# A 3x3 convolution on one core: dealing output channels to partitions so that sixteen DMA engines store neighbouring channels

## The chip, the core and the metric

The kernel runs on one core of a Trainium2 chip. The core has a matrix engine (TensorE, PE in the profile), a vector engine (VectorE, DVE), a scalar engine (ScalarE, ACT), a general engine (GpSimd, POOL) and SyncE (SP), which in this kernel issues every transfer. Transfers between the chip's memory and the on-chip memory of 128 partitions are carried out by sixteen DMA engines that work beside the others. The metric is the device time of one execution in microseconds (us); less is better. The median of three executions of the kernel before is 126.97 us (126.95 to 127.01).

## The reference

The inputs are 16 images of 64 channels with 64 x 64 points, and the weights of a 3 x 3 convolution from 64 to 128 channels, all in 32-bit floats:

```
x: (16, 64, 64, 64)      weight: (128, 64, 3, 3) * 0.1
x_pad = pad(x, one zero on each side of h and w)
output[b, co] += weight[co, ci, kh, kw] * x_pad[b, ci, kh:kh+h, kw:kw+w]     (sum over ci, kh, kw)
output: (16, 128, 64, 64), float32
```

The input holds 16.8 MB and the output 33.6 MB. One channel of one image is 64 x 64 x 4 = 16,384 bytes, and lies in one piece in memory; the channels of an image follow each other.

## The kernel before

**Tiling.** Two images make a pair `p` (0 to 7); their 2 x 64 input channels fill the 128 partitions. Each pair is worked on in two halves `h` of 32 output rows, so there are sixteen steps of the main loop (line 221). The rows are transformed in the manner of Winograd along the height: two output rows come from sums and differences of input rows (`ss`, `dd`, `ee`, made on GpSimd two steps ahead; `xh`, a cast to 16 bits on ScalarE) and combined weights `Wt`. TensorE multiplies for the two images of a pair with 64 rows each, and the products for image `b2` land in an accumulator of 128 output channels. VectorE (lines 247 to 251) and ScalarE (lines 192 and 253) put the four parts together in the output tile `ov[b2]`, whose partition is the output channel.

**Weights.** The first transfer (line 59) loads the weights as 128 rows of 2,304 bytes, row `co` into partition `co` of `w_raw`. They are cast, transposed by matmuls with an identity (line 102) and combined to `Wt`. Which output channel sits in which partition of the accumulators, and then of the output tiles, follows from which weight row was loaded into which partition of `w_raw`.

**Loads.** Pair 0 comes in two transfers (34 and 30 rows), pairs 1 and 2 in one each, pairs 3 and 4 together in one transfer into a double tile `two` (line 81). Pairs 5, 6 and 7 are loaded later, when a tile comes free (`NEXT_LOADS`): after the steps (1, 1), (3, 0) and (4, 0).

**Homes.** `X_HOME` and `O_HOME` say in which of five single and two double tiles a pair's input and outputs lie. An output tile is used again for a later pair, so the later pair's results wait until the earlier store has landed.

**Stores.** After the second half of a pair `store` (line 204) issues its stores. For the pairs in `BOTH` (0, 3 and 6) one transfer stores both images: for each partition, the channel of the first image and then that of the second, 2 MB further on. The other pairs are stored by two transfers of 128 channels. One image, the second of pair 5, is cut (`FEW`): its first 57 rows go as usual, and its last 7 rows are stored by a transfer of 124 partitions and one of 4, so that the packets are 7 x 64 x 4 = 1,792 bytes.

**What sets the order.** `keep` fixes each engine's instructions in the order of the text. All transfers are issued by SyncE in that order: a transfer that waits for results holds up those behind it. The DMA engines work each through its own list of packets in the order of issue. The completion of a transfer is told by one of eight flags that the framework takes in turn, so that a transfer also waits until the one eight places before it has landed. The order of transfers is: weights, pair 0 in two parts, 1, 2, 3 and 4; stores of pairs 0 and 1; load of 5; store of 2; load of 6; store of 3; load of 7; stores of 4, 5, 6, 7.

Of the kernel before, what the change touches and what calls it, by code (L numbers as in the profile page):

```python
# [15 lines left out]
def kernel(  # L16
# [12 lines left out]
    nc = tc.nc  # L29
    B, CI, H, W = x.shape  # L30
    CO = weight.shape[0]
# [3 lines left out]

    keep = tc.keep_in_program_order
    x_rows = x.rearrange("b c h w -> (b c) h w")
    w_flat = weight.rearrange("co ci kh kw -> co (ci kh kw)")

    const = ctx.enter_context(tc.tile_pool(name="const", bufs=1))  # L40
    psum = ctx.enter_context(tc.tile_pool(name="psum", bufs=8, space=bass.MemoryType.PSUM))
# [6 lines left out]

    X_HOME = [0, 1, 2, ("d", 0), ("d", 1), 2, ("d", 0), ("d", 1)]
    O_HOME = ["b", (3, 4), (0, 1), "b", (3, 4), (0, 1), "b", (2, 3)]  # L50
    BOTH = (0, 3, 6)
    FEW = 5, 1, 7
    NEXT_LOADS = {(1, 1): 5, (3, 0): 6, (4, 0): 7}

    def home(k, name):
        return slots.tile([128, H, W], F32, tag=f"s{k}", name=name)

    w_raw = const.tile([CO, CI * 9], F32)
    keep(nc.sync.dma_start(w_raw, w_flat))
    xs = {}  # L60

    def load(p, cuts=((0, H),)):
        if X_HOME[p] in range(5):
            xs[p] = home(X_HOME[p], "xs")
        for lo, hi in cuts:
            keep(
                nc.sync.dma_start(
                    xs[p][:, lo:hi, :], x_rows[128 * p : 128 * p + 128, lo:hi, :]
                )
            )  # L70

    two = slots.tile([128, 2, H, W], F32, tag="d", name="two")
# [4 lines left out]
    load(0, ((0, 34), (34, H)))  # L77
    load(1)
    load(2)
    rows = x_rows[128 * 3 : 128 * 5, :, :].rearrange("(g p) h w -> p g h w", g=2)  # L80
    keep(nc.sync.dma_start(two, rows))

    ident = const.tile([128, 128], F16)
    make_identity(nc, ident)
# [45 lines left out]
    def cast(p, h):  # L130
        t = cpool.tile([128, 17, W], F16, tag="xh", name="xh")
        keep(nc.scalar.copy(t, xs[p][:, C_ROW[h] : C_ROW[h] + 17, :]))  # L132
        return t

    def transforms(eng, p, h):
        return sums(eng, p, h), diffs(eng, p, h), outers(eng, p, h)
# [17 lines left out]
    def mms(tiles, terms, start, stop):  # L154
        n = 3 * len(terms)
        i = 0
        for wi, src, row in terms:
            for kw in (1, 0, 2):
                c_lo, c_hi = max(0, 1 - kw), min(W, W + 1 - kw)
                lo, hi = 0, RB  # L160
                at, step, rows = row
                while at + step * lo < 0:
                    lo += 1
                while at + step * (hi - 1) > rows - 1:
                    hi -= 1
                first, last = at + step * lo, at + step * (hi - 1)
                for b2 in range(2):
                    p0 = 64 * b2
                    keep(
                        nc.tensor.matmul(  # L170
                            tiles[b2][:, lo:hi, c_lo:c_hi],
                            Wt[p0 : p0 + 64, wi, kw, :],
                            src[
                                p0 : p0 + 64,
                                first : last + 1 : step,
                                c_lo + kw - 1 : c_hi + kw - 1,
                            ],
                            start=start and i == 0,
                            stop=stop and i == n - 1,
                            skip_group_check=not start,  # L180
                        )
                    )
                i += 1

    def acc():
        return [psum.tile([128, RB, W], F32, tag="acc", name="acc") for _ in range(2)]

    def copies(tiles):
        us = []
        for b2 in range(2):  # L190
            ut = upool.tile([128, RB, W], F32, tag="ut", name="ut")
            keep(nc.scalar.copy(ut, tiles[b2]))  # L192
            us.append(ut)
        return us
# [3 lines left out]
    def outputs(p):  # L198
        if O_HOME[p] == "b":
            both = slots.tile([128, 2, H, W], F32, tag="b", name="both")  # L200
            return both, [both[:, b2, :, :] for b2 in range(2)]
        return None, [home(k, "ot") for k in O_HOME[p]]

    def store(p, both, ots):
        if p in BOTH:
            pair = out[2 * p : 2 * p + 2, :, :, :].rearrange("b c h w -> c b h w")
            keep(nc.sync.dma_start(pair, both))
            return
        for b2 in range(2):
            parts = [(0, CO, 0, H)]  # L210
            if (p, b2) == FEW[:2]:
                at = H - FEW[2]
                parts = [(0, CO, 0, at), (0, 124, at, H), (124, 4, at, H)]
            for c, n, lo, hi in parts:
                keep(
                    nc.sync.dma_start(
                        out[2 * p + b2, c : c + n, lo:hi, :], ots[b2][c : c + n, lo:hi, :]
                    )
                )

    for n, (p, h) in enumerate(halves):
        if n + 2 < len(halves):
            tr[halves[n + 2]] = transforms(nc.gpsimd, *halves[n + 2])
        if h == 0:
            both, ots = outputs(p)
            ov = [t.rearrange("p (j i) c -> p j i c", i=2) for t in ots]
        ss, dd, ee = tr.pop((p, h))
        xc = xh.pop((p, h))
        jf, jg = RB * F_BLK[h], RB * G_BLK[h]
        sf, sg = jf - 16 * h, jg - 16 * h  # L230
        g_at = 2 * jg - C_ROW[h]

        pf1, pg1, pf2, pg2 = acc(), acc(), acc(), acc()
        mms(pf1, [(HP, ss, (sf, 1, 16))], True, True)
        ux = copies(pf1)
        mms(pg1, [(G1, ss, (sg, 1, 16))], True, True)
        ug = copies(pg1)
        mms(pf2, [(HM, dd, (0, 1, RB))], True, True)
        uy = copies(pf2)
        if n + 1 < len(halves):  # L240
            xh[halves[n + 1]] = cast(*halves[n + 1])
        mms(pg2, [(G01, xc, (g_at, 2, 17)), (G2, xc, (g_at + 2, 2, 17))], True, True)
        mms(pf1, [(G0, ee, (0, 2, 16))], False, True)
        mms(pg1, [(G21, xc, (g_at + 1, 2, 17)), (G0, xc, (g_at - 1, 2, 17))], False, True)
        mms(pf2, [(G2, ee, (1, 2, 16))], False, True)
        for b2 in range(2):
            keep(nc.vector.tensor_add(ov[b2][:, jg : jg + RB, 1, :], pg2[b2], ug[b2]))  # L247
        for b2 in range(2):
            keep(nc.vector.tensor_add(ov[b2][:, jf : jf + RB, 0, :], pf1[b2], uy[b2]))  # L249
        for b2 in range(2):  # L250
            keep(nc.vector.tensor_sub(ov[b2][:, jf : jf + RB, 1, :], ux[b2], pf2[b2]))  # L251
        for b2 in range(2):
            keep(nc.scalar.copy(ov[b2][:, jg : jg + RB, 0, :], pg1[b2]))  # L253
        if h == 1:
            store(p, both, ots)
        if (p, h) in NEXT_LOADS:
            load(NEXT_LOADS[p, h])

# [29 lines left out]
```

## Time and profile before

| what | value |
|---|---|
| median of three executions | 126.97 us |
| the profiled execution | 127.13 us |
| its span (first to last instruction) | 125.4 us |
| PE, DVE, ACT, POOL busy | 95.6, 66.8, 85.4, 90.5 us |
| moved | 50.78 MB, mean 405 GB/s |
| read from, written to memory | 17.07 MB, 33.55 MB |
| transfers issued by SyncE | 24: 9 loads (the weights among them), 15 stores |

The page gives busy time by engine, the span in 40 slices (a digit is a tenth of a slice; the row DMA is the mean of the sixteen DMA engines, GB/s what they moved), the DMA queues, and the chain of work that ended last. The queue q1 carries the kernel's transfers; q8 and q14 carry the engines' program code. Beside the page the trace holds a record of every packet that a DMA engine moved, with start, duration and size; in this kernel a packet of a whole channel has 16,384 bytes. The completion of a transfer shows as sixteen packets of 4 bytes, one on each engine that took part.

### The profile page before, as it was taken

How to read it: one execution, taken by the hardware profiler on the slowest of the kernel's cores; microseconds unless marked ns; L12 is line 12 of the kernel's file. 1: busy time of each engine (PE TensorE's matmuls, PEld its weight loads, DVE VectorE, ACT ScalarE, POOL GpSimd, SP SyncE). 2: the span in 40 equal slices, each digit the busy share in tenths (PEclk: the TensorE clock that was granted, in tenths of full speed). 3: DMA queues.
4: the chain of work that ended last, by engine and by line, in shares of the span. 5: the costliest groups of instructions: out<-in, count | busy, mean ns of one | idle time of the engine just before them, and what ended most of it. 6: DMA issues, size and time to landing. Idle time of an engine off the chain costs nothing.

```text
span 125.4 us, 2343 instructions
## 1 busy us (share of the span) xinstructions
PE 95.6 (76%) x873; PEld 48.9 (39%) x873; DVE 66.8 (53%) x104; ACT 85.4 (68%) x150; POOL 90.5 (72%) x52
## 2 busy tenths in 40 slices
PE   0349999999999999999999999999999960000000
PEld 0223555555455555555555555555555520000000
DVE  0199658393939476574939394765749390000000
ACT  4458598989797988989897979789898930000000
POOL 2209999999999999999999999999999300000000
PEclk9999999999999999999999999999999996555555
DMA  4999999999999999999999999999999999999971
GB/s 132 371 453 423 434 424 439 423 335 418 434 431 429 426 434 418 423 429 434 416 439 424 423 423 423 418 431 434 423 424 423 433 416 443 423 429 444 418 335 47
DMA packets 3827, 50.78 MB, mean 405 GB/s; under 512 B 360, under 2 KB 488, under 8 KB 744
## 3 DMA queue, kind: packets, MB, share of 16 engines
q1 hardware_dynamic: 3816, 50.63, 96.2%
q8 instruction: 7, 0.11, 0.3%
q14 instruction: 4, 0.03, 0.1%
HBM read 17.07 MB, written 33.55 MB: 404 GB/s over the span
## 4 chain that ended last, share of the span: by engine, by line
PE 76%; DMA 2%; DVE 2%; POOL 1%; DVEq 0%; ACT 0%; issue 0%
PE acc L170 75%; DMA w_raw<-in_weight_dram 2%; DVE ss L114 1%; DVE ot L251 1%; POOL w L87 1%; DVEq L283 0%; DVE th L141 0%; DVE Wt L142 0%; PE wp L102 0%; ACT g0h L139 0%; DVEq L142 0%
## 5 line engine op out<-in xcount | busy, mean ns | idle before, releaser
L170 PEld LDWEIGHTS <-Wt 64*128 64x128 f16 x864 | 48.0, 96 | 48.5 <-issue 3.0
L192 ACT COPY ut<-acc 128x512 f32<-128x512 f32 x96 | 48.7, 612 | 4.4 <-PE acc L170 4.4
L170 PE MATMUL acc<-xh,Wt 64*128 64x504 f16 (+3 forms) x384 | 46.2, 372 | 0.0
L170 PE MATMUL acc<-ss,Wt 64*128 64x504 f16 (+1 forms) x192 | 24.8, 392 | 2.3 <-DVE ss L114 2.3
L170 PE MATMUL acc<-ee,Wt 64*128 64x504 f16 (+1 forms) x192 | 26.4, 377 | 0.0
L247 DVE TENSOR_TENSOR ot<-acc,ut 128x512 f32<-128x512 f32 x20 | 12.9, 686 | 20.0 <-ACT ut L192 15.8
L114 POOL TENSOR_TENSOR ss<-xs 128x1024 f16<-128x1024 f32 x7 | 16.6, 2366 | 4.7 <-DMA xs<-in_x_dram 4.7
L127 POOL TENSOR_TENSOR ee<-two 128x1024 f16<-128x1024 f32 x8 | 19.0, 2378 | 0.0
L114 POOL TENSOR_TENSOR ss<-two 128x1024 f16<-128x1024 f32 x8 | 19.0, 2369 | 0.0
L127 POOL TENSOR_TENSOR ee<-xs 128x1024 f16<-128x1024 f32 x7 | 16.6, 2376 | 0.0
L253 ACT COPY ot<-acc 128x512 f32<-128x512 f32 x20 | 10.7, 589 | 5.5 <-PE acc L170 5.5
L170 PE MATMUL acc<-dd,Wt 64*128 64x504 f16 (+1 forms) x96 | 13.9, 392 | 0.0
L247 DVE TENSOR_TENSOR both<-acc,ut 128x512 f32<-128x512 f32 x12 | 7.7, 686 | 11.0 <-ACT ut L192 7.9
L251 DVE TENSOR_TENSOR ot<-ut,acc 128x512 f32<-128x512 f32 x20 | 12.8, 682 | 0.2
L249 DVE TENSOR_TENSOR ot<-acc,ut 128x512 f32<-128x512 f32 x20 | 12.8, 680 | 0.0
L121 POOL TENSOR_TENSOR dd<-two 128x512 f16<-128x512 f32 x8 | 10.3, 1287 | 0.0
L121 POOL TENSOR_TENSOR dd<-xs 128x512 f16<-128x512 f32 x7 | 10.0, 1423 | 0.0
L132 ACT CAST xh<-two 128x1088 f16<-128x1088 f32 x8 | 9.3, 1157 | 0.0
L132 ACT CAST xh<-xs 128x1088 f16<-128x1088 f32 x8 | 9.2, 1145 | 0.0
L253 ACT COPY both<-acc 128x512 f32<-128x512 f32 x12 | 6.4, 589 | 3.5 <-PE acc L170 3.5
L251 DVE TENSOR_TENSOR both<-ut,acc 128x512 f32<-128x512 f32 x12 | 7.7, 683 | 0.1
L249 DVE TENSOR_TENSOR both<-acc,ut 128x512 f32<-128x512 f32 x12 | 7.7, 680 | 0.0
(23 smaller groups left out, 14.9 us busy)
## 6 DMA issues: line engine op xcount, KB each, us to landing
out_dram<-ot SPq DMA_DIRECT2D x9, 2048.0 KB, 18.5
out_dram<-both SPq DMA_DIRECT2D x3, 4096.0 KB, 22.5
xs<-in_x_dram SPq DMA_DIRECT2D x3, 2048.0 KB, 16.2
two<-in_x_dram SPq DMA_DIRECT2D x1, 4096.0 KB, 28.4
two<-in_x_dram SPq DMA_DIRECT2D x2, 2048.0 KB, 23.1
out_dram<-ot SPq DMA_DIRECT2D x1, 1824.0 KB, 24.3
xs<-in_x_dram SPq DMA_DIRECT2D x1, 1088.0 KB, 5.4
xs<-in_x_dram SPq DMA_DIRECT2D x1, 960.0 KB, 7.4
```

The costliest lines, as they stand in the source:

```text
L87: keep(nc.gpsimd.tensor_copy(w16[:, 0, :], w_raw))
L114: keep(eng.tensor_add(t, v[:, j : j + 16, 0, :], v[:, j : j + 16, 1, :]))
L121: keep(eng.tensor_sub(t, v[:, j : j + RB, 1, :], v[:, j : j + RB, 0, :]))
L127: keep(eng.tensor_sub(t, xs[p][:, r - 1 : r + 15, :], xs[p][:, r + 1 : r + 17, :]))
L132: keep(nc.scalar.copy(t, xs[p][:, C_ROW[h] : C_ROW[h] + 17, :]))
L170: nc.tensor.matmul(tiles[b2][:, lo:hi, c_lo:c_hi], Wt[p0 : p0 + 64, wi, kw, :], src[p0 : p0 + 64, first : last + 1 : step, c_lo + kw - 1 : ...
L192: keep(nc.scalar.copy(ut, tiles[b2]))
L247: keep(nc.vector.tensor_add(ov[b2][:, jg : jg + RB, 1, :], pg2[b2], ug[b2]))
L249: keep(nc.vector.tensor_add(ov[b2][:, jf : jf + RB, 0, :], pf1[b2], uy[b2]))
L251: keep(nc.vector.tensor_sub(ov[b2][:, jf : jf + RB, 1, :], ux[b2], pf2[b2]))
L253: keep(nc.scalar.copy(ov[b2][:, jg : jg + RB, 0, :], pg1[b2]))
```

## The change

- Weight row `16 j + e` is loaded into partition `8 e + j` (e from 0 to 15, j from 0 to 7), so partition `8 e + j` of every output tile holds output channel `16 j + e`.
- A store of an image is written as 16 x 8 channels in memory, `e` outside and `j` inside, from 128 partitions. If a DMA engine takes one `e`, that is eight neighbouring partitions, then at its step `j` the sixteen engines store the sixteen neighbouring channels `16 j` to `16 j + 15`.
- No transfer stores a pair: pairs 0, 3 and 6 are stored by two transfers each as well. Pairs 3 and 4 are loaded by two transfers.
- The images of the last pair are stored in two halves of 32 rows each (`HALVED`), by transfers of 8,192-byte packets.
- The last 7 rows of pair 5's second image are stored by four transfers of 4 x 8 channels (32 partitions each) instead of 124 and 4 partitions.

```diff
-    w_flat = weight.rearrange("co ci kh kw -> co (ci kh kw)")
+    w_dealt = weight.rearrange("(j e) ci kh kw -> e j (ci kh kw)", e=16)
...
-    BOTH = (0, 3, 6)
+    HALVED = (7,)
...
-    keep(nc.sync.dma_start(w_raw, w_flat))
+    keep(nc.sync.dma_start(w_raw, w_dealt))
...
-    rows = x_rows[128 * 3 : 128 * 5, :, :].rearrange("(g p) h w -> p g h w", g=2)
-    keep(nc.sync.dma_start(two, rows))
+    load(3)
+    load(4)
...
-            return both, [both[:, b2, :, :] for b2 in range(2)]
-        return None, [home(k, "ot") for k in O_HOME[p]]
-
-    def store(p, both, ots):
-        if p in BOTH:
-            pair = out[2 * p : 2 * p + 2, :, :, :].rearrange("b c h w -> c b h w")
-            keep(nc.sync.dma_start(pair, both))
-            return
-        for b2 in range(2):
-            parts = [(0, CO, 0, H)]
+            return [both[:, b2, :, :] for b2 in range(2)]
+        return [home(k, "ot") for k in O_HOME[p]]
+
+    def store(p, ots):
+        for b2 in range(2):
+            to = out[2 * p + b2].rearrange("(j e) h w -> e j h w", e=16)
+            cuts = [0, 32, H] if p in HALVED else [0, H]
             if (p, b2) == FEW[:2]:
-                at = H - FEW[2]
-                parts = [(0, CO, 0, at), (0, 124, at, H), (124, 4, at, H)]
-            for c, n, lo, hi in parts:
+                cuts = [0, H - FEW[2]]
+            for lo, hi in zip(cuts, cuts[1:]):
+                keep(nc.sync.dma_start(to[:, :, lo:hi, :], ots[b2][:, lo:hi, :]))
+
+            for g in range(0, 16, 4) if cuts[-1] < H else ():
                 keep(
                     nc.sync.dma_start(
-                        out[2 * p + b2, c : c + n, lo:hi, :], ots[b2][c : c + n, lo:hi, :]
+                        to[g : g + 4, :, cuts[-1] : H, :],
+                        ots[b2][8 * g : 8 * g + 32, cuts[-1] : H, :],
                     )
                 )
...
-            store(p, both, ots)
+            store(p, ots)
```

More of the change, by code (lines that the diff above doesn't have):

```diff
@@ L224 @@
         if h == 0:
-            both, ots = outputs(p)
+            ots = outputs(p)
             ov = [t.rearrange("p (j i) c -> p j i c", i=2) for t in ots]
```

## The prediction

> **What bounds the kernel now.** I read the page's slices first, then the chain of waits, then SyncE's waits, then the windows, and last the trace's records of single DMA packets.
>
> ```profile
> span 125.4 us, 2343 instructions
> ...
> DMA  4999999999999999999999999999999999999971
> GB/s 132 371 453 423 434 424 439 423 335 418 434 431 429 426 434 418 423 429 434 416 439 424 423 423 423 418 431 434 423 424 423 433 416 443 423 429 444 418 335 47
> ...
> q1 hardware_dynamic: 3816, 50.63, 96.2%
> q8 instruction: 7, 0.11, 0.3%
> ```
>
> The DMA engines are full from the second slice to the last but one; no compute engine is busy after slice 33. The chain's last pieces and SyncE's waits say the same:
>
> ```profile
> 8.00 94.44 PE acc L170 x864
> 102.44 0.68 DVE ot L251
> 103.12 0.60 DVEq L283
> ```
>
> ```profile
> SPq L283 <- DMA out_dram<-ot: 9.9, 3, 4.8
> SPq L283 <- DMA out_dram<-both: 9.6, 1, 9.6
> SPq L67 <- ACT xh L132: 7.9, 3, 3.0
> ```
>
> The last result is computed at 103.1 us, the last store issued right after, and the remaining 21 us are SyncE at the end of the program waiting for stores. TensorE's 76% of the span is beside the point: what ends the kernel is 50.63 MB through sixteen DMA engines. The windows give their rate by stage (last column GB/s, the one before the engines' busy share):
>
> ```profile
> 2.00:8.00 6.00, 1.15 (x9) 1.02 (x10) 2.30 (x4) 2.69 (x6) 0.66 (x1) 1.00 1.00 381
> 8.00:26.00 18.00, 18.00 (x149) 8.80 (x150) 12.89 (x19) 14.58 (x27) 16.86 (x9) 1.00 1.02 434
> 26.00:29.00 3.00, 3.00 (x32) 1.59 (x30) 2.90 (x5) 2.34 (x5) 3.00 (x2) 1.00 0.99 322
> 29.00:47.00 18.00, 18.00 (x172) 9.24 (x170) 11.21 (x18) 16.02 (x30) 18.00 (x10) 1.00 1.01 430
> 68.00:76.00 8.00, 8.00 (x78) 4.08 (x76) 4.93 (x8) 7.12 (x14) 8.00 (x5) 1.00 0.99 420
> 82.00:103.00 21.00, 20.41 (x192) 10.29 (x188) 14.23 (x23) 17.46 (x32) 16.28 (x9) 1.00 1.01 427
> 104.00:118.00 14.00, 0.00 (x0) 0.00 (x0) 0.00 (x0) 0.00 (x0) 0.00 (x0) 0.52 1.01 432
> ```
>
> Loads alone run at 434, stores alone at 430 to 432. The packet records say why: the median 16 KB packet takes 611 ns in every stage, load or store (all 365 that start from 8 to 22 us, 329 of 367 from 104 to 118), and the next starts 4 ns before it ends, so one per 607 ns per engine, 27.0 GB/s, 432 for sixteen. A store already moves at an engine's own pace, wherever its channels lie. What is not at that pace: the 3 us around 28 us, where the first loads end and the first store begins, lose (432 - 322) x 3 / 432 = 0.76 us; the windows from 29 to 103 us lose 0.86 us together by the same working; and the engines end apart, their last completions lying between 120.2 and 124.2 us with a mean of 122.1. The late one fits seven fetches of TensorE's code (the q8 line, 16 KB each, 0.88 to 1.04 us, each beside one data packet stretched to about 1.0 to 1.1): 7 x 0.607 = 4.2 us against a spread of 4.0.
>
> **The change part by part.** The profiled execution took 127.13 us (span 125.4 and 1.8 around it), 0.16 above the median of 126.97. The sum is made on it and the 0.16 taken off.
>
> *Same work.* All matmuls, copies and transforms stay, in the same order on their engines. Weight rows are permuted as they are loaded, so a result lands in another partition at the same instruction. Bytes are the same. These cost nothing, and need no cover.
>
> *Weight load.* Still 128 rows of 2,304 B, now 36,864 B apart for one engine. It heads the DMA queue and the chain (0.74 to 3.69 us), so a delay moves everything. Records: median 93 ns, worst 552. Bounds: one such worst packet more or less, plus or minus 0.46 us; I take 0, since each engine's first packets are slow now (164 to 552 ns) and the sixteen rows of one step are neighbours as well.
>
> *Pairs 3 and 4 loaded by two transfers instead of one, pairs 0, 3 and 6 stored by two instead of one, the last two images by two halves each.* Six more transfers on all sixteen engines. The end of a transfer costs an engine 6 ns: the completions of consecutive loads lie 4.862 us apart for 8 packets of 607 ns (4.856). 6 x 6 = 0.04 us. The halved images have 8 KB packets: the records have 328 ns for 8,704 B and 291 for 7,680, so 309.5 for 8,192; two are 619 against 611. Starts lie 4 ns closer, so between 3.4 and 8 ns for each of 16 packets; I take 3.4, the start-to-start value: 0.05 us.
>
> *The seven rows that four engines store alone.* Before 31 + 1 packets of 1,792 B on each, after 4 x 8 = 32; two more transfer ends, 0.01 us. The 128 packets took 74 ns each, and this share stays.
>
> *Issues.* Eight more transfers on SyncE, at 0.39 us each (the three-dimensional store of a pair took 383 to 405 ns, against 356 for a plain one): 3.1 us. SyncE waits 78 us for VectorE at its stores, and the queue it feeds is 10 to 20 us deep (18.5 us median from issue to landing): hidden. At its thinnest, pair 1's store is issued at 34.14 us, 3.8 us before pair 0's is through at 37.9. The last four issues end near 105.5 us; the first engine is through with the previous pair at 110.4: cover 4.9 us.
>
> *Waits.* Eight completion flags are taken in turn, so each transfer waits for the one eight before it. More transfers make that one a later one. The tight ones, by landings in the trace: the fourth piece of the seven rows waits for the load of pair 7 (last engine 85.8 us; issued before at about 82.8); pair 6's second image waits for pair 4's second (95.5, against 92.27); the last pair's second half for pair 5's second image (104.7, against 103.2). Behind each on SyncE stand only later stores, and nothing computes from them. Each comes over 4 us before an engine could use it: 0. Output tiles are reused no later: pair 6 needs pair 3's store, landed by 80.9 us, as before.
>
> *Where a store reads and writes.* This is the substance, and the trace of before does not show it. On the memory side the sixteen engines now fill 256 KB without gaps at a step. The nearest rows: loads of the same rows at 434 GB/s, stores at 432. Since both are at the engine's pace, a better pattern can take away only the excess listed above: at most 0.76 + 0.86 = 1.62 us. A worse one is bounded by the slowest 8 us of the trace, 420 against 432 GB/s: 33.55 MB of stores, 77.7 us, times 2.8% = 2.2 us, of which about 0.6 is paid already: 1.6 us. I take 0, between equal ends and nearest to the 611 ns median. On the on-chip side each engine should now read eight neighbouring partitions. Nearest row: the seven rows. Four engines sweep over 31 partitions each, between 100.9 and 103.9 us, while the others read their own partitions; every small packet took 74 ns, and of 97 large packets then in flight 85 took their usual 545 or 611. Reading near another engine cost nothing there, for short stretches.
> [...]
>
> The sum: 127.13 + 0.04 + 0.05 + 0.01 = 127.23, less 0.16: 127.07; I say 127.1.
>
> **The rivals.**
> *The stall at the switch shrinks (faster).* In its favour: the stall is shared by nearly all engines at once (29 packets between 25.9 and 29.2 us took over 660 ns), and stores by pair alternate between two images 2 MB apart, which stops. Against: it falls on the last two packets of the loads, which the change leaves, and later switches (near 52, 67 and 82 us) cost little. Half of the 1.62 us gone: 127.07 - 0.8 = 126.3.
> *Neighbouring blocks get into each other's way in memory (slower).* Place: every store packet. Price: half the bound, 0.8 us, so 127.9. It decides from 2 ns on each of an engine's 128 store packets (0.25 us). For it: some store packets from 30 to 47 us already take 640 to 660 ns (mean 615.4). Against: the loads from 8 to 22 us read neighbouring rows with no slow packet at all.
> *Two engines share a way out of on-chip memory (much slower).* Place: every store of all sixteen engines. If the shared way carries what one engine moves, a packet takes 2 x 607 ns and the 77.7 us of stores double: 205 us; engines that drift four packets apart would escape it, and the late one is six or seven behind. Against: the 74 ns. [...]
> *The split is another one.* If an engine gets other partitions than eight neighbours, a step stores some groups of channels apart. The time is then the forecast's.
>
> **How the numbers follow.** No change apart from the 0.1 us, with the other split in it: 0.34, range 126.8 to 127.3. Stall shrinks: 0.26. Memory conflict: 0.30. Shared way: 0.10. A measurement of this kernel tells from no change about 0.2%, 0.25 us. So faster 0.26, same 0.34, slower 0.40. The range 126.2 to 128.4 leaves out the shared way (0.10), the upper end of the memory conflict (0.03) and the best part of the gain (0.06).
>
> **What would show it.** Right: 16 KB store packets with a median of 611 ns, 8 KB near 309; 104 to 118 us still at about 432 GB/s; 26 to 29 near 322; SyncE's last waits still on stores of some 20 us. Wrong: store stages under 425 (conflict) or near 216 (shared way), packets of 1.2 us; 26 to 29 us above 380 (gain); TensorE with gaps before 102 us, which would mean that a flag wait or a late load reached the computation.

## The result: 10.5% slower, and the profile after

The changed kernel takes 140.99 us (median of six executions, 139.63 to 143.62), the kernel before on the same chip 126.99. The ratio is 1.105, with a 95% interval of 1.099 to 1.111. Medians here and below are of all executions, while ratios leave out those more than 1.5% above the fastest of their kernel, here two of the six. The forecast was 127.1 with a range from 126.2 to 128.4: wrong. The profiled execution took 139.97 us. Its slices, as on the page:

```profile
span 138.1 us, 2357 instructions
...
DMA  3999999999999999999999999999999999999851
GB/s 105 377 449 437 427 427 427 408 384 280 299 316 363 365 351 380 318 418 432 434 408 403 418 422 403 377 413 413 427 422 420 411 390 351 335 318 346 337 242 55
...
q1 hardware_dynamic: 4176, 50.63, 94.6%
```

The same bytes, the DMA engines just as busy, and yet 280 to 365 GB/s in twelve of the forty slices: from the first store on, and again near the end. The windows that answer to those of the kernel before (the last column is GB/s):

```profile
2.00:8.00 6.00, 1.15 (x9) 1.02 (x10) 1.41 (x3) 1.81 (x5) 0.66 (x1) 1.00 0.96 356
8.00:26.00 18.00, 17.12 (x146) 8.49 (x147) 13.12 (x19) 15.05 (x28) 16.21 (x8) 1.00 1.02 433
26.00:29.00 3.00, 3.00 (x32) 1.61 (x30) 3.00 (x6) 2.34 (x4) 3.00 (x3) 1.00 1.02 382
29.00:47.00 18.00, 18.00 (x172) 9.36 (x170) 11.53 (x19) 16.02 (x30) 18.00 (x10) 1.00 1.00 329
68.00:76.00 8.00, 7.38 (x67) 3.44 (x65) 4.36 (x8) 6.55 (x13) 7.43 (x4) 1.00 1.01 412
82.00:103.00 21.00, 18.55 (x153) 8.86 (x154) 8.95 (x16) 14.41 (x25) 18.16 (x11) 0.92 1.00 408
104.00:118.00 14.00, 6.00 (x57) 2.79 (x51) 5.17 (x9) 4.68 (x10) 2.22 (x1) 0.88 1.02 391
```

Loads are untouched (433 against 434 from 8 to 26 us). The pure store stage from 29 to 47 us fell from 430 to 329. The engines show as fully busy in it (share 1.00 at 329 GB/s, 1.01 at 430 before): a slow packet counts as busy for the whole of its duration, so the share cannot tell a slow engine from a full one; the last column can. The packet records show 226 packets of 16 KB over 950 ns, 93 of them at 1.1 to 1.3 us and 49 longer, against 24 before. Over what packets of their size usually take, the records of an engine add up to about 12.2 us on the average, against 2.2: 10.0 us more. That is most of the 12.8 us by which the last completion moved (136.9 against 124.2 us); 0.44 us are at the head of the queue, shown below; the rest was not taken apart.

The chain's longest pieces and SyncE's and VectorE's waits show what the slow stores drew after them:

```profile
8.88 47.94 PE acc L171 x432
58.20 31.21 DMA out_dram<-both
90.95 16.91 PE acc L171 x136
```

```profile
SPq L212 <- DMA out_dram<-ot: 17.0, 4, 4.7
SPq L284 <- DMA out_dram<-ot: 9.6, 4, 2.4
SPq L284 <- DMA out_dram<-both: 8.3, 1, 8.3
...
SPq L216 <- DMA two<-in_x_dram: 4.2, 1, 4.2
```

```profile
DVE both L248 <- DMA out_dram<-both: 7.4, 1, 7.4
```

VectorE now waits 7.4 us until pair 3's store has landed, since pair 6 goes into the same tile, and the computation ends at 110.5 us instead of 103.1. SyncE waits 17.0 us for flags of earlier stores. Both are consequences: in every microsecond from 90 to 126 at least fifteen of the sixteen engines had a packet under way on the average, so these waits did not leave the queue empty.

### The profile page after: what moved, and what is told of

It is laid out like the page before. It is cut to its first block, busy times and chain, and to the rows that moved or that the text cites. A ratio compares the mean times of both kernels' runs of the same rounds, so it can differ in the third digit from the quotient of the medians.

```text
span 138.1 us, 2357 instructions
## 1 busy us (share of the span) xinstructions
PE 98.3 (71%) x873; PEld 49.6 (36%) x873; DVE 66.5 (48%) x104; ACT 85.7 (62%) x150; POOL 90.6 (66%) x52
## 4 chain that ended last, share of the span: by engine, by line
PE 47%; DMA 25%; DVE 4%; issue 1%; DVEq 1%; ACT 0%; POOL 0%; ACTq 0%
PE acc L171 47%; DMA out_dram<-both 23%; DMA w_raw<-in_weight_dram 3%; DVE ot L250 1%; DVE ss L115 1%; DVE both L248 1%; DVE ot L252 0%; DVE both L252 0%; POOL w L88 0%; DVEq L284 0%; DVE th L142 0%; DVE Wt L143 0%; PE wp L103 0%; ACT g0h L140 0%; ACT ut L193 0%
## 5 line engine op out<-in xcount | busy, mean ns | idle before, releaser
L171 PEld LDWEIGHTS <-Wt 64*128 64x128 f16 x864 | 48.7, 96 | 54.5 <-issue 8.7
L171 PE MATMUL acc<-xh,Wt 64*128 64x504 f16 (+3 forms) x384 | 47.4, 370 | 0.0
L171 PE MATMUL acc<-ss,Wt 64*128 64x504 f16 (+1 forms) x192 | 27.5, 406 | 6.2 <-DVE ss L115 2.3
L171 PE MATMUL acc<-ee,Wt 64*128 64x504 f16 (+1 forms) x192 | 27.9, 377 | 0.1
L171 PE MATMUL acc<-dd,Wt 64*128 64x504 f16 (+1 forms) x96 | 15.0, 400 | 0.0
L252 DVE TENSOR_TENSOR ot<-ut,acc 128x512 f32<-128x512 f32 x20 | 12.8, 682 | 0.2
L250 DVE TENSOR_TENSOR ot<-acc,ut 128x512 f32<-128x512 f32 x20 | 12.8, 681 | 0.0
```

Source lines behind the costliest of these rows:

```text
L171: nc.tensor.matmul(tiles[b2][:, lo:hi, c_lo:c_hi], Wt[p0 : p0 + 64, wi, kw, :], src[p0 : p0 + 64, first : last + 1 : step, c_lo + kw - 1 : ...
```

## The experiments

Ratios are to runs of the kernel before on the same chip. Theory A: with the store written as 16 x 8, an engine reads eight neighbouring partitions, and engines whose partitions lie 32 apart share one way out of on-chip memory. Theory B: sixteen neighbouring channels collide in memory. Theory C: more transfers on eight flags hold the queue up. A "way" below means such a shared way out. The three are conjectures; the records show durations, starts and sizes of packets, no way and no engine.

### Single stores, one after the other

```diff
+    src = const.tile([128, 8, 4100], F32)
...
+        "wide": src[32:93:4, :, 0:4096],
+        "eight": src[0:61:4, :, 0:4096],
+        "four": src[0:16, :, 0:4096],
...
+    for to, data in stores:
+        keep(nc.sync.dma_start(to, data))
+        keep(nc.vector.memset(src[:, 0, 0:1], 1.0))
```

> This kernel leaves the convolution out: it fills a tile with ones and stores it sixteen times, one store after the other, 2 MiB each, sixteen engines with 8 packets of 16 KB. Theory A (two engines that read partitions 32 apart at the same time share one way out of on-chip memory): the plain 128-partition stores take 4.9 us of packets (611 ns each); the stores in the changed kernel's shape take 9.7 us (1.2 us a packet, as all engines start together); of the stores from sixteen single partitions, those from partitions 32, 36, ... 92 take 4.9 us, those from 0, 4, ... 60 (eight pairs 32 apart) 9.7 us, those from 0 to 15 (four to a quadruple) 19 us, each whether the sixteen engines write neighbouring channels or channels eight apart. Shapes 64 x 2 and 32 x 4: 9.7 us if they are cut into the same blocks of eight partitions. Theory B (neighbouring channels collide in memory): every store to neighbouring channels is slow, from whichever partitions, and every store to channels eight apart takes 4.9 us.

Windows of this run, each laid around one store (the last column is GB/s over the window, its edges included): the plain store; the store in the changed kernel's shape; partitions 32 to 92 to channels eight apart, then to neighbours; partitions 0 to 60 to channels eight apart, then to neighbours; partitions 0 to 15; shape 64 x 2; shape 32 x 4.

```profile
36.00:41.00 5.00, 0.00 (x0) 0.00 (x0) 1.00 0.94 397
43.00:52.50 9.50, 0.00 (x0) 0.00 (x0) 1.00 0.88 204
72.50:77.50 5.00, 0.00 (x0) 0.00 (x0) 1.00 0.97 410
79.50:84.50 5.00, 0.00 (x0) 0.00 (x0) 1.00 0.92 387
86.50:96.50 10.00, 0.00 (x0) 0.00 (x0) 1.00 0.94 197
98.50:108.50 10.00, 0.00 (x0) 0.00 (x0) 1.00 0.94 197
148.50:169.00 20.50, 0.00 (x0) 0.00 (x0) 1.00 0.91 94
193.00:198.00 5.00, 0.00 (x0) 0.00 (x0) 1.00 0.89 377
199.80:204.80 5.00, 0.00 (x0) 0.00 (x0) 1.00 0.94 397
```

From first to last packet the stores took 5.08 us (plain), 9.80 (changed shape), 5.09 and 5.09 (partitions 32 to 92), 10.33 and 10.33 (partitions 0 to 60), 20.66 (partitions 0 to 15), 5.07 and 5.07 (64 x 2 and 32 x 4); the second copies of the first six agree within 0.01 us. In this run the partitions that sixteen engines read decide, and where the channels lie in memory changes nothing: 5.09 against 5.09, 10.33 against 10.33. Theory B falls. Shifting the same sixteen partitions by 32 halves the time. From partitions 0 to 60 a store takes 2.03 times the 5.09 us, from 0 to 15 4.06 times. The times lie 1 to 9% above theory A's. One expectation missed: the shapes 64 x 2 and 32 x 4 also store neighbouring channels, and run at the full rate, so by theory A they are not cut into blocks of eight partitions as 16 x 8 is. How they are cut was not measured.

The packets of the store in the changed shape show that the engines do not stay in step. The records do not name the engine, but the sixteen fifth packets can be told: they start together, 5.03 to 5.23 us into the store, as the fourth ones end. Durations in ns, the first line in order of start:

```
fifth packets, changed shape:           611 1134 611 611 611 1198 1141 1028 1142 611 611 1016 975 787 669 611
second to seventh, partitions 0 to 60:  1267 to 1288
```

With the fifth packet seven engines run at 611 ns, five of them for their next packet too, and so get ahead of the others; from partitions 0 to 60, where an engine reads one partition throughout, none does. That an engine comes to another way after its fourth partition is the author's reading of this and of the factor 4.06 for partitions 0 to 15. Why the seven get ahead is open: all sixteen fifth packets start within 0.2 us, so the lead is more than the time in which, by this reading, the new way could have been empty.

### The change without its core

```diff
-    BOTH = (0, 3, 6)
+    HALVED = (7,)
...
+    load(3)
+    load(4)
...
-            parts = [(0, CO, 0, H)]
+            parts = [(0, CO, 0, 32), (0, CO, 32, H)] if p in HALVED else [(0, CO, 0, H)]
```

> The change without its core: pairs 3 and 4 loaded apart, no pair stored by one transfer, the last pair in halves, but plain weights and plain stores of 128 partitions, and the seven rows as before. Theories A and B: as before, 126.8 to 127.5 us. Theory C (more transfers on eight flags hold the queue up): 133 to 141 us.

127.52 us, ratio 0.999 (0.994 to 1.003). Six of the eight additional transfers, the halves and the later flag waits cost nothing that this can tell; the seven rows are in two pieces here, not four. Theory C falls.

### Setting engines apart in the kernel

```diff
-    load(4)
+    for c, n in (0, 36), (36, 12), (48, 4), (52, 4), (56, 4), (60, 4), (64, 64):
+        r = 128 * 4 + c
+        keep(nc.sync.dma_start(xs[4][c : c + n], x_rows[r : r + n]))
```

> The changed kernel with the seven rows stored like the rest, and pair 4 loaded by transfers of 36, 12, 4, 4, 4, 4 and 64 partitions, by which engines 0 to 3 should move 12 packets, 4 to 11 eight and 12 to 15 four: engines 0 to 3 then run four packets behind 4 to 7, and 8 to 11 four behind 12 to 15, so that two engines 32 partitions apart are never on the same four partitions' way. Theory A: the slow packets go, 127.5 to 130 us (engines 0 to 3 end 2.4 us late, about what the seven rows cost them before). Theories B and C: 138 to 142 us, as the changed kernel.

> As offset_pairs, but pair 4 is loaded by four transfers of 8 partitions and one of 96: engines 0 to 7 move ten packets and 8 to 15 six, so engines are four packets apart, but none of the pairs 0 and 4, 1 and 5 and so on. Theory A: as slow as the changed kernel, 137 to 143 us. If any spread among the engines would do (they collide in memory because all are at the same step): 128 to 131 us.

The first has a median of 147.66 us (ratio 1.136, 1.125 to 1.147) and missed upward; the second has 143.26, its four executions lying between 140.30 and 145.43. The comparison tells nothing: the loads in small pieces are slow themselves. The windows from 18 to 30 us, first of the one with seven pieces, then of the one with five (profiled at 143.76 us):

```profile
18.00:30.00 12.00, 12.00 (x116) 6.12 (x112) 7.99 (x13) 10.68 (x20) 12.00 (x7) 1.00 1.03 298
```

```profile
18.00:30.00 12.00, 12.00 (x116) 6.14 (x114) 7.50 (x12) 10.68 (x20) 12.00 (x7) 1.00 1.04 265
```

In the same window the kernel before has 404, the changed kernel 410. Each small piece is 4, 8 or 12 neighbouring partitions, and the probe's store from sixteen neighbouring ones took 20.66 us instead of 5.09, so the pieces may have collided on the way in; that was not measured apart.

### Setting engines apart, second and third try

The next kernel stores ones again, four images back to back.

```diff
+    group([], (4, 5, 6, 7))
+    group([(0, 12, src[32:80:4]), (48, 4, src[32:48:4])], (8, 9, 10, 11))
+    group([(64, 8, src[32:64:4])], (12, 13, 14, 15))
```

> This kernel leaves the convolution out: it stores ones. Three groups, each begun when the one before has landed. Each stores four images in the changed kernel's shape back to back (32 packets an engine). The first group begins with all engines together. The second begins with stores from partitions that lie on ways of their own, 4 packets on twelve engines and 4 more on four, so that engines 0 to 3 start the images four packets behind 4 to 7, and 8 to 11 four behind 12 to 15. The third begins with 4 packets on engines 0 to 7. Theory A (pairs 32 partitions apart share a way, and collide as long as they step together): first group 28 to 40 us, second 22 to 26 us (40 packets on the fullest engines at 607 ns are 24.3), third 30 to 42 us. If engines 32 partitions apart are not what collides: second as slow as the first.

The groups took 32.1, 32.5 and 32.5 us. The second missed its 22 to 26 and was as slow as the first, which is what was expected if engines 32 partitions apart were not what collides. It began faster (292 GB/s in its first 10 us against 238 in the first group). A possible reason for the miss is that its small stores read partitions, such as 64 and 32, that by theory A lie on the ways of engines already at their images, so that they lost the lead that they were to make; this was not measured. The run decides nothing either way. The windows of the first group, 10, 10 and 11.6 us, show the rate rise from 238 to 300 GB/s, as it would if the engines fall out of step (the last one holds the end of the group):

```profile
36.40:46.40 10.00, 0.00 (x0) 0.00 (x0) 1.00 0.99 238
46.40:56.40 10.00, 0.00 (x0) 0.00 (x0) 1.00 1.00 300
56.40:68.00 11.60, 0.00 (x0) 0.00 (x0) 1.00 0.65 251
```

The third try sets apart half of the pairs only, and from partitions that by theory A collide with nobody:

```diff
+        group([], (b, b + 1))
+        group([(16 * k, 4, src[4:32:8])], (b + 2, b + 3))
+        group([(32 + 32 * k, 8, src[0:32:4])], (b + 4, b + 5))
```

> This kernel leaves the convolution out: it stores ones. Six groups, each begun when the one before has landed, three kinds twice over; each stores two images in the changed kernel's shape (16 packets an engine). Kind 1: nothing ahead. Kind 2: ahead of them 4 packets on engines 0 to 3 from partitions 4, 12, 20 and 28, which no engine reads in the first half of an image, so that engines 0 to 3 start four packets behind 4 to 7 and nothing collides on the way there; engines 8 to 15 are left as they are. Kind 3: 4 packets on engines 0 to 7 from partitions 0, 4, ... 28, which sets no pair apart. Theory A (only the pairs 0 and 4, 1 and 5 ... 11 and 15 collide, while they are on the same four partitions): in kind 2 engines 0 to 7 run at 611 ns throughout, so at least 140 of 272 packets take under 660 ns; in kind 1 fewer than a third of 256 (one image alone: about a sixth), in kind 3 32 more than in kind 1. If any collision among sixteen neighbouring channels were the cause, the shares of kinds 2 and 3 would be alike.

| kind | packets | under 660 ns | us |
|---|---|---|---|
| 1, nothing ahead | 256 | 67 and 66 | 18.5 and 18.5 |
| 2, engines 0 to 3 four packets back | 272 | 150 and 152 | 17.8 and 17.7 |
| 3, engines 0 to 7 four packets back | 288 | 99 and 99 | 20.2 and 20.1 |

The counts are as theory A had them: the store meant to set the pairs 0 and 4 to 3 and 7 apart by half an image brings 150 and 152 fast packets instead of 67 and 66, the one meant to set eight engines back together frees nobody (99 is 67 plus the 32 of the small store). In kind 2 engines 0 to 7 were not at 611 ns throughout, as had been expected: their 144 packets and half of kind 1's 67 would make 177 fast ones, and 150 and 152 were counted. Where the lead falls short was not seen. The group's length hardly falls; the other eight engines, left as they were, may end it.

### Neighbouring channels without the shared way

```diff
-    w_dealt = weight.rearrange("(j e) ci kh kw -> e j (ci kh kw)", e=16)
+    w_dealt = weight.rearrange("(j e) ci kh kw -> e j (ci kh kw)", e=64)
...
-            to = out[2 * p + b2].rearrange("(j e) h w -> e j h w", e=16)
+            to = out[2 * p + b2].rearrange("(j e) h w -> e j h w", e=64)
```

> The changed kernel with channels dealt over 64 instead of 16: partition 2 e + j holds channel 64 j + e, stores of 64 x 2; the seven rows are stored like the rest. Theory A, with the lone store of this shape at full rate: the slow packets go; as plain_nofew within 0.3%, 126.8 to 128 us. If neighbouring channels help at all, 125.5 to 126.5.

> As plain_rest, with the seven rows stored like the rest: the control of deal64. The engines on which they were get 2.4 us less, all others 0.54 us more: 127.0 to 127.8 us, since the latest engine is one of the others.

128.57 us, ratio 1.011 (1.008 to 1.014), for the channels dealt over 64; 127.92 us, ratio 1.007 (1.005 to 1.009), for the plain control. Both medians lie above what was expected (128 and 127.8), and the dealt one 0.5% above its control, not within 0.3%. The kernel dealt over 64 differs in this one number from the changed kernel without its seven rows, which is measured below at a ratio of 1.090: the slow packets are gone, 25 over 950 ns against 165 in that kernel. Nothing is gained from neighbours: the store stage runs at 426 against 428 GB/s. Windows of the kernel dealt over 64, of the control, and of the kernel dealt over 16 without the seven rows:

```profile
0.00:2.00 2.00, 0.00 (x0) 0.00 (x0) 0.00 (x0) 1.27 (x1) 0.70 (x6) 1.00 0.00 0
29.00:47.00 18.00, 18.00 (x172) 9.10 (x170) 11.21 (x18) 16.03 (x29) 18.00 (x10) 1.00 1.00 426
```

```profile
0.00:2.00 2.00, 0.00 (x0) 0.00 (x0) 0.00 (x0) 1.27 (x1) 0.70 (x6) 1.00 0.11 29
29.00:47.00 18.00, 18.00 (x172) 9.15 (x170) 11.21 (x18) 16.02 (x30) 18.00 (x10) 1.00 1.01 428
```

```profile
29.00:47.00 18.00, 18.00 (x172) 9.05 (x168) 11.95 (x21) 15.80 (x30) 18.00 (x11) 1.00 1.00 334
```

The 0.65 us between the dealt kernel and the control lies mostly in the first row: with dealt weights no byte moves in the first 2 us. The issue of the weight load takes 0.66 us with dealt rows against 0.37 (SyncE's timeline), and its first packet starts at 2.17 us against 1.74. All six profiled convolutions with dealt weights start at 2.17 to 2.19 us, all four with plain weights at 1.73 to 1.75.

### The seven rows and the halves

```diff
-    FEW = 5, 1, 7
+    FEW = 5, 1, 11
```

> The kernel before with eleven rows instead of seven stored by four engines alone: the twelve others get 4 x 76 ns less, the four 4 x 227 ns more. If the four still end before the latest engine: 126.6 to 126.8 us (0.3 us faster); if not, up to 127.4.

127.65 us, ratio 1.003 (1.0005 to 1.005): slightly slower, and with its median above even the 127.4 of the less favoured expectation. The latest completion moved from 124.2 to 124.7 us. Together with the control above (none of these rows: 1.007) seven is the best of the three.

The next two are the changed kernel itself with `FEW` off, and with `HALVED = ()`.

> The changed kernel with the seven rows of pair 5 stored like the rest. If the seven rows, which put engines 0 to 3 some four packets back, bring pairs that had drifted four apart into step again: the stage after 115 us stays above 380 GB/s instead of 326, and the time falls to 136 to 139 us. If they have no part in it: 141 to 142 us, the seven rows' own worth of 0.7% more.

> The changed kernel with the last pair stored in whole images. If the 8 KB halves are neutral, as the 0.1 us of the prediction: 139.5 to 142 us. If halving itself costs (eight more flag waits at the end): 1 us or more below the changed kernel.

138.80 us, ratio 1.090 (1.077 to 1.102), and 141.99 us, ratio 1.103 (1.089 to 1.118). The halves are neutral within these intervals. Whether the seven rows bring pairs back into step is not settled. The time without them is in the expected 136 to 139, but its interval overlaps that of the changed kernel. The stage from 115 to 125 us rose only to 368 GB/s, below the expected 380, and stood at 370 in the profile with the rows and without the halves, against 326 in the changed kernel. For the rows speak the packets of 16 KB over 950 ns that start after 110 us: 55 in the changed kernel, 46 without the halves, 7 without the rows. Against them, the 8 KB packets over 500 ns are 32 with the rows and 49 without. Each is one profile. The windows of the changed kernel, without the rows, and without the halves:

```profile
115.00:125.00 10.00, 0.00 (x0) 0.00 (x0) 0.00 (x0) 0.00 (x0) 0.00 (x0) 0.50 0.98 326
```

```profile
115.00:125.00 10.00, 0.00 (x0) 0.00 (x0) 0.00 (x0) 0.00 (x0) 0.00 (x0) 0.50 0.99 368
```

```profile
115.00:125.00 10.00, 0.00 (x0) 0.00 (x0) 0.00 (x0) 0.00 (x0) 0.00 (x0) 0.50 1.00 370
```

## Why the prediction was wrong

- **What bounds the kernel: right.** The DMA engines, with a median of 611 ns for a whole channel in both profiles, set the end before and after: the last completions come at 124.2 and 136.9 us, the last results at 103.1 and 110.5.
- **"Where a store reads and writes", on-chip side: wrong, and this is the step that failed.** It took 0 from the row of the seven rows: 74 ns each while others read. That row was short and not alike. (Of the large packets beside it, 82 by the records rather than 97, 72 took 545 or 611 ns.) Its 128 packets of 1,792 B spread over 3 us; by theory A each way was met for a few of them only, while the change puts pairs on one way for four packets of 16 KB at a stretch, for every store. The probe measured what stood in question: 1.28 us a packet instead of 0.61. That the old trace could not show a sustained share should have kept the price open there, as the text did for the memory side.
- **The rival "two engines share a way out": right in place, and the runs fit its mechanism; its price was wrong, and its chance of 0.10 too low.** When it was put on record no row stood behind the sharing or behind its four packets; the probe's 1.28 us a packet, and kind 2's 150 fast packets against 67, came after. It doubled all stores: 205 us. It said that engines four packets apart escape, and gave that only to the late one. In fact many engines fall out of step by themselves (seven of the sixteen fifth packets of the probe take 611 ns), and the rate rises (329 to 425 GB/s). What was left was 10.0 us of slow packets on top of the 77.7 us of stores.
- **Memory side: 0, right.** Neighbouring channels neither help nor hurt (5.09 against 5.09 us; 426 against 428 GB/s). So the rivals "neighbouring blocks get into each other's way" and "the stall shrinks" have nothing to stand on; the first switch did run at 382 GB/s in the changed kernel against 322, a gain of 0.4 us, but the kernel dealt over 64 has 317 and the plain control 295 there, so neighbours are not its cause; what is, stays open.
- **Six more transfers, halves, issues, flags: right within what can be told** (ratio 0.999, interval 0.994 to 1.003). Even in the changed kernel, where SyncE waited 17 us longer for flags, the DMA engines did not run empty (at least fifteen of sixteen had a packet under way on the average from 90 to 126 us). "Output tiles are reused no later" did not hold there: pair 3's store landed at 89.4 us instead of 80.9 and held VectorE up for 7.4 us, as a consequence of the slow stores.
- **Weight load: 0 taken, 0.44 us measured** to its first packet, inside the bound of 0.46, but by another cause than the packets considered: 0.3 of it is the issue itself, 0.66 to 0.68 us against 0.37 to 0.38. By its landing the bound did not hold: the weights were in at 4.57 us instead of 3.69, with one packet of 1,066 ns. And the kernel dealt over 64 as a whole is 0.65 us above its control.
- **"The split is another one": not so for 16 x 8** (the probe's change of pace at the fifth packet and the pairs freed in kind 2 both fit blocks of eight), but so, by theory A and the full rate (5.07 us), for 64 x 2 and 32 x 4. The split itself shows in no record.

## What to carry to other kernels

In these runs the partitions that sixteen engines read at a step set the time of a 2 MiB store: 5.09 us from 32, 36, ... 92, 10.33 from 0, 4, ... 60, 20.66 from 0 to 15. How the memory side is written can halve the rate of a store that moves the same bytes: 9.80 us as 16 x 8, 5.07 as 64 x 2, presumably because the partitions are dealt to engines in another way. When DMA engines show as busy, read GB/s and the packets' durations beside it: the share stood at 1.00 over 329 GB/s and at 1.01 over 430. And a row that shows a resource shared for moments is no bound for sharing it throughout: leave the price open and give the mechanism its chance.

## What had not been expected of the hardware

- The engines of a 16 x 8 store do not stay in step. A single store in the 16 x 8 shape takes 9.80 us where partitions 0, 4, ... 60 take 10.33, four back to back take 32.1 instead of four times 9.8, and in the kernel the rate rises from 329 GB/s (29 to 47 us) to 425 (62 to 68 us), with the load of pair 5 between. It is back at 326 from 115 to 125 us; why is open.
- A load whose memory side is dealt is issued later: 0.3 us more on SyncE for 128 rows of weights, the first packet 0.44 us later, in all ten profiles of the convolution.
- Stores of 64 x 2 and 32 x 4 run at the plain rate (5.07 us), a 16 x 8 store of the same channels at about half (9.80 us). At which shape between 16 x 8 and 32 x 4 the time changes was not tried.
